# A two-layer decoder trunk on one core: where running sums join the residual, how the first input is loaded, and when heads are transposed

## The chip, the cores and the metric

The kernel runs on one core of a Trainium2 chip. The metric is the device time of one execution in microseconds (us). The kernel before took 2208.25 us, the median of three runs (2207.6, 2208.25 and 2216.12 us).

## What is computed

A residual stream x of 256 positions and 2048 channels (float32) goes through two layers and a final RMSNorm. Cut to what matters here:

```
for l in range(DEPTH):                      # DEPTH = 2
    h    = rms_norm(x, attn_norm_g[l])
    proj = h @ w_in[l]                      # 2048 -> 5632: q, k, v of two attention groups, su, sv
    mix  = concat(moba_attention(...),      # 6 heads of 128
                  diff_attention(...),      # 6 heads, two softmaxes each, RMSNorm per head
                  spatial_gating(gelu(su), gelu(sv)))
    x = x + mix @ w_out[l]
    h = rms_norm(x, mlp_norm_g[l])
    x = x + square(relu(h @ w_mlp_in[l])) @ w_mlp_out[l]     # 2048 -> 8192 -> 2048
return rms_norm(x, final_norm_g)
```

## The kernel before, in words

**Splitting.** Every float32 weight tile is split into a high and a low part of the matmul format (`weights`, lines 102 to 121, and `halves`): ScalarE (ACT) copies the high part, `hi_*`, and VectorE (DVE) subtracts it from the raw tile to give the low part, `lo_*`. Activations are split likewise. A product is then three matmuls of 512 columns: high by high, low by high, high by low. The raw tiles have three buffers, the split ones four of two k steps each, so that the splitting runs ahead of TensorE (PE) by at most eight k steps. All weights are loaded from SyncE's queue (SP).

**The two matmul routines.** `gemm` (line 138) makes 2 x 512 columns of a plain product in two of the four PSUM banks of the pool `psg`. `gemm7` (line 181) makes 2 x 1024 columns with seven products in place of eight for the first 1536 rows of the weights' k range (tiles `b11`, `t1`, `t2`, `b22`, `t3`, `t4`, `b21`), and the remaining rows plainly (`plain`). It uses all four banks, px, py, pz and pw. px and py gather running sums: at four points the running content is saved with `keep` (`s1`, `s5`, `v2`, `v3`), and the bank goes on collecting. At its end the four blocks are the banks plus such saved sums. Between the k steps both routines call `pump()`, which takes one step of a pending generator (`mixing`, the heads, `turn`, `hidden`, `gate`); with two or more pending, the first two take turns.

**The MLP.** The hidden width is cut in four chunks, c = 0 to 3. Each has two `gemm7` of the first matrix (names ending in h) and two of the second (names ending in o), 32 in the two layers, 16 of them o. In an o gemm `keep` (lines 681 to 685) has ACT evict the running sum from PSUM, scaled by `r2` or its negative, to a tile `kept`, and has GpSimd (POOL) start a DMA that adds this tile to the residual `xt` in SBUF. At the end DVE adds each bank times `r2` to `xt` (lines 688 to 691), in the order py, pw, pz, px. In an h gemm `keep` (lines 657 to 663) keeps the sums on chip, and `v3` is a subtraction on DVE, `s5` minus px. The tiles `kept` have four buffers that h and o share.

**The attention part.** For each layer `gemm` first makes the columns sv (line 345 or 354), then the groups 8, 7, ..., 0, 9 of the input projection (`wi`). Between sv and group 8 stand the sums of squares of x, 1/rms (`rstd`), small loads and the eviction of sv's banks (`svz`, line 401). In layer 0 x itself (`xt`, two loads of 1 MB) and the small loads (idt, mask, rope, lng, lnb, lam, swt) stand on SP's queue between the loads of sv and those of group 8. `differential` (line 484) is a generator of six steps for one head: in its fifth step PE multiplies by v, ACT squares, DVE and POOL make 1/rms and ACT scales; in the sixth PE transposes the result (`poT`, line 516).

**The order** of instructions on each engine is fixed at compile time by the framework's scheduler from the order of the program and its own estimates, so an instruction may stand a few places from where the program has it. Each engine works through its own list.

Of the kernel before, what the change touches and what calls it, by code (L numbers as in the profile page):

```python
# [11 lines left out]
AF = mybir.ActivationFunctionType  # L12
ALU = mybir.AluOpType
# [3 lines left out]
P = 128  # L17
# [9 lines left out]
GW = 512  # L27
NG = D // GW
FCH = 4
# [12 lines left out]
def trunk(ctx: ExitStack, tc: tile.TileContext, x_in, xT, w_in, w_out, w_mlp_in, w_mlp_out,  # L42
          cols, sgu_wT, ln_g, ln_b, fin_g, lam, rope, mask, ident, out):
    nc = tc.nc
    V, A, G, T = nc.vector, nc.scalar, nc.gpsimd, nc.tensor
# [22 lines left out]
    def bank(name, tag="m"):  # L68
        return psa.tile([P, GW], F32, tag=tag, name=name)


    xt = [cpool.tile([P, D], F32, name=f"xt{t}") for t in range(2)]
# [61 lines left out]
    def drain():  # L134
        while pending:
            pump()

    def gemm(w, order, c0, lhs, name, sizes=(4, 4, 4, 4), before=None):

        ps = [psg.tile([P, GW], F32, tag="g", name=f"pg{t}_{name}") for t in range(2)]  # L140
        i = 0
        for size in sizes:
            ks = order[i:i + size]
            if before:
                before(ks)
            for k, (hi, lo) in zip(ks, weights(w, ks, c0, f"{name}_{i}")):
                a, j = lhs[k]
                first, last = i == 0, i == len(order) - 1
                i += 1
                for t in range(2):  # L150
                    ah, al = a[:, j, t * P:(t + 1) * P], a[:, j, S + t * P:S + (t + 1) * P]
                    T.matmul(ps[t], lhsT=ah, rhs=hi, start=first, stop=False)  # L152
                    T.matmul(ps[t], lhsT=al, rhs=hi, start=False, stop=False)  # L153
                    T.matmul(ps[t], lhsT=ah, rhs=lo, start=False, stop=last)  # L154
                pump()
        return ps
# [161 lines left out]
    xa = [None] * KT  # L318

    def load_x(ks):  # L320
# [5 lines left out]
        for i, k in enumerate(ks):  # L326
# [2 lines left out]
            split(d[:, k % 2], x0[:, i, :], col(C_ATT + k))  # L329
            xa[k] = (d, k % 2)  # L330

    ss_a = None
    for l in range(DEPTH):
        lam_init = 0.8 - 0.6 * math.exp(-0.3 * l)
        wi, wo, w1, w2 = w_in[l], w_out[l], w_mlp_in[l], w_mlp_out[l]
        allk = list(range(KT))
# [6 lines left out]

        if l == 0:
            psv = gemm(wi, allk, SV * P, xa, "sv0", sizes=(2, 2, 4, 4, 4), before=load_x)
            for t in range(2):
                nc.sync.dma_start(xt[t], x_in[t * P:(t + 1) * P, :])
            nc.sync.dma_start(idt, ident)
            ss_a = sums("a0")
            for t in range(2):  # L350
                for g in range(NG):
                    square_sum(ss_a, t, g, "a0")
        else:
            psv = gemm(wi, allk, SV * P, xa, f"sv{l}")
        drain()
        nc.sync.dma_start(maskt, mask)
        nc.sync.dma_start(ropet, rope)
# [126 lines left out]
        def differential(h):  # L484
            n = f"d{l}{h}"
            qk = turned_qk("d", h, n)
            yield
            e0, s0 = softmax(scores(qk, slice(0, 64), n + "a"), 0.125, n + "a")
            yield
            e1, s1 = softmax(scores(qk, slice(64, 128), n + "b"), 0.125, n + "b")  # L490
            V.tensor_scalar(s1, s1, nlam, None, op0=ALU.mult)
            for j, (a, b) in enumerate(((0, P), (P, 3 * P))):
                A.activation(e0[:, a:b], e0[:, a:b], AF.Copy, scale=s0[:, j:j + 1])
                V.scalar_tensor_tensor(e0[:, a:b], e1[:, a:b], s1[:, j:j + 1], e0[:, a:b],
                                       op0=ALU.mult, op1=ALU.add)
            yield
            pt = probs_t(e0, n)
            vs = vh["d", h]
            yield
            po = bank(f"po_{n}")  # L500
            T.matmul(po[:, 0:P], lhsT=pt[:, 0:P], rhs=vs[0], start=True, stop=True)
            T.matmul(po[:, P:S], lhsT=pt[:, P:S], rhs=vs[0], start=True, stop=False)
            T.matmul(po[:, P:S], lhsT=pt[:, S:3 * P], rhs=vs[1], start=False, stop=True)
            o = t1(f"o_{n}")
            ssq = small.tile([P, 2], F32, tag="ssq", name=f"ssq_{n}")
            for t in range(2):
                A.activation(o[:, t * P:(t + 1) * P], po[:, t * P:(t + 1) * P], AF.Square,
                             accum_out=ssq[:, t:t + 1])
            V.tensor_scalar(ssq, ssq, 1.0 / P, EPS, op0=ALU.mult, op1=ALU.add)
            G.tensor_tensor(ssq, ssq, mhalf[:, :2], op=ALU.pow)  # L510
            for t in range(2):
                A.activation(o[:, t * P:(t + 1) * P], po[:, t * P:(t + 1) * P], AF.Copy, scale=ssq[:, t:t + 1])
            yield
            pT = bank(f"poT_{n}")
            for t in range(2):
                T.transpose(pT[:, t * P:(t + 1) * P], o[:, t * P:(t + 1) * P], idt)
            split(mix_half(6 + h), pT[:, :S], gsub)
# [67 lines left out]

        pending.append(mixing())
        for g in (8, 7, 6, 5, 4, 3, 2, 1, 0, 9):
            ps = gemm(wi, allk, g * GW, xa, f"wi{l}{g}")
            if g == 9:
                pending.append(gate(ps))  # L590
            else:
                take(g, ps)
            for h in {5: (2, 3, 4, 5), 4: (0, 1)}.get(g, ()):
                pending.append(differential(h))
            for h in {1: (4, 5), 0: (0, 1, 2, 3)}.get(g, ()):
                pending.append(block_attention(h))
# [14 lines left out]
        for g in range(NG):  # L611
            ps = gemm(wo, order, g * GW, Late(), f"wo{l}{g}")
# [13 lines left out]
        xa = [None] * KT  # L626
# [25 lines left out]
        for c in range(FCH):  # L652
            hid, hs = [None] * KT, [None] * SP
            for g in range(2):
                kept = {}

                def keep(what, ps, kept=kept, n=f"{l}{c}{g}"):
                    k = mlp.tile([P, GW], F32, tag="kept", name=f"k{what}h{n}", bufs=4)
                    if what == "v3":
                        V.tensor_tensor(k, kept["s5"], ps, op=ALU.subtract)  # L660
                    else:
                        A.activation(k, ps, AF.Copy)
                    kept[what] = k

                ps = gemm7(w1, c * fw + 2 * g * GW, Want(xm), Want(xs), allk[2 * SP:], keep, f"h{l}{c}{g}")
                z11, z12, z22 = kept["s1"], kept["v2"], kept["v3"]
                V.scalar_tensor_tensor(z12, z12, -1.0, ps[0][1], op0=ALU.mult, op1=ALU.add)
                V.tensor_tensor(z22, z22, ps[1][1], op=ALU.add)
                pending.append(hidden(hid, hs, ((z12, z12), (z22, z22)), 8 * g + 4, f"hid{l}{c}{g}b"))
                V.tensor_tensor(z11, z11, ps[0][0], op=ALU.add)  # L670
                pending.append(hidden(hid, hs, ((z11, z11), (ps[1][0], None)), 8 * g, f"hid{l}{c}{g}a"))
                if r2 is None:
                    rm = rstd(ss_m, f"m{l}")
                    r2 = small.tile([P, 4], F32, tag="r2", name=f"r2_{l}", bufs=2)
                    V.tensor_tensor(r2[:, :2], rm, rm, op=ALU.mult)
                    V.tensor_scalar(r2[:, 2:], r2[:, :2], -1.0, None, op0=ALU.mult)
            for g in range(2):
                def xg(t, half, g=g):
                    return xt[t][:, (2 * g + half) * GW:(2 * g + half + 1) * GW]

                def keep(what, ps, g=g, n=f"{l}{c}{g}"):
                    t, half, sign = {"s1": (0, 0, 0), "v2": (0, 1, 2), "s5": (1, 1, 0), "v3": (1, 1, 2)}[what]
                    k = mlp.tile([P, GW], F32, tag="kept", name=f"k{what}o{n}", bufs=4)
                    A.activation(k, ps, AF.Copy, scale=r2[:, sign + t:sign + t + 1])
                    G.dma_start(xg(t, half, g), k, accum_op=ALU.add)

                ps = gemm7(w2[c * fw:(c + 1) * fw], 2 * g * GW, Want(hid), Want(hs), late, keep, f"o{l}{c}{g}")
                for half in (1, 0):
                    for t in range(2):
                        V.scalar_tensor_tensor(xg(t, half), ps[t][half], r2[:, t:t + 1], xg(t, half),  # L690
                                               op0=ALU.mult, op1=ALU.add)
                        if c == FCH - 1:
                            square_sum(ss_a, t, 2 * g + half, f"n{l}")
                    if c == FCH - 1 and not fin:
                        q = 2 * g + half
                        pending.append(turn(xa, xt, q * GW, 4 * q, f"xa{l + 1}_{q}_", C_ATT + (l + 1) * KT))
# [75 lines left out]
```

## Time and profile before

| | before |
|---|---|
| median of 3 runs | 2208.25 us |
| the profiled execution | 2210.08 us |
| its span, first to last instruction | 2208.4 us |
| mean granted TensorE clock | 0.993 |
| PE busy with matmuls | 2148.7 us (97%) |
| DVE busy | 1614.9 us (73%) |
| ACT busy | 1312.5 us (59%) |
| POOL busy | 74.0 us (3%) |
| DMA, mean rate over the span | 191 GB/s |
| HBM read | 402.23 MB |

All times in the profile are microseconds from the start of the span unless they are marked ns. Matmuls overlap, and their ends are modelled: a matmul of 512 columns is recorded as 0.39 us long while the next starts 0.23 us after it. So "busy" is no peak, and a gap of PE between a recorded end and the next start is shorter than the time really lost. [...]

### The profile page before, as it was taken

What the parts mean: (1) busy time and instruction counts of PE and PEld (TensorE: products, weight loads), DVE (VectorE), ACT (ScalarE), POOL (GpSimd) and SP (SyncE); (2) the same over time, 40 slices, a digit from 0 to 9 for tenths busy, and PEclk for the clock granted to TensorE, in tenths of its full rate; (3) what the DMA queues carried; (4) which work ended last, traced back from release to release, by engine and by line L of the source; (5) the groups of instructions that cost most, each with busy time, mean ns of one, the idle gap of its engine ahead of it and who ended that gap; (6) DMA issues with size and microseconds to landing.
All of it is one profiled execution on the core that took longest, in us unless ns stands there. A gap on an engine that the chain in (4) does not pass through costs nothing. (4 is left out here: it accounts for less than half of the span.)

```text
span 2208.4 us, 26211 instructions
## 1 busy us (share of the span) xinstructions
PE 2148.7 (97%) x9596; PEld 1731.0 (78%) x9596; DVE 1614.9 (73%) x2040; ACT 1312.5 (59%) x1935; POOL 74.0 (3%) x90
## 2 busy tenths in 40 slices
PE   8999999999999999999999999999999999999997
PEld 6877888887787787788888778888878877877885
DVE  6555665897788787788765655668868977887876
ACT  6456465675566565566663655656656755755764
POOL 0000000000000000000000000000000000000000
PEclk9999999999999999999999999999999999999999
DMA  8544565467656666657666444645765676566564
GB/s 294 189 153 139 174 221 181 153 189 222 196 194 197 200 200 208 187 185 223 186 205 196 145 152 156 227 143 183 223 204 191 190 227 209 178 200 208 194 214 124
DMA packets 214385, 422.82 MB, mean 191 GB/s; under 512 B 9840, under 2 KB 10480, under 8 KB 213872
## 3 DMA queue, kind: packets, MB, share of 16 engines
q1 hardware_dynamic: 204176, 402.23, 55.5%
q0 software_dynamic: 9216, 16.78, 4.3%
q10 hardware_dynamic: 864, 2.14, 0.3%
q8 instruction: 75, 1.23, 0.2%
q14 instruction: 54, 0.44, 0.1%
HBM read 402.23 MB, written 2.10 MB: 183 GB/s over the span
## 5 line engine op out<-in xcount | busy, mean ns | idle before, releaser
L119 DVE TENSOR_TENSOR lo_wi<-raw_wi,hi_wi 128x1024 fp32r<-128x1024 f32 x160 | 195.6, 1223 | 177.7 <-ACT hi_wi L118 177.5
L118 ACT ACTIVATE hi_wi<-raw_wi 128x1024 fp32r<-128x1024 f32 x160 | 169.1, 1059 | 182.4 <-PE pg_wi L153 176.1
L118 ACT ACTIVATE hi_o<-raw_o 128x1024 fp32r<-128x1024 f32 x160 | 168.5, 1060 | 171.8 <-PE px_o L221 103.3
L152 PE MATMUL pg_wi<-hi_wi,xa 128*128 128x512 f32 x640 | 261.8, 409 | 4.3 <-ACT hi_wi L118 4.3
L154 PE MATMUL pg_wi<-lo_wi,xa 128*128 128x512 f32 x640 | 253.0, 395 | 1.0 <-DVE lo_wi L119 1.0
L153 PE MATMUL pg_wi<-hi_wi,xa 128*128 128x512 f32 x640 | 252.8, 395 | 0.0
L119 DVE TENSOR_TENSOR lo_h<-raw_h,hi_h 128x1024 fp32r<-128x1024 f32 x160 | 193.0, 1222 | 59.5 <-ACT hi_h L118 59.5
L118 ACT ACTIVATE hi_h<-raw_h 128x1024 fp32r<-128x1024 f32 x160 | 168.4, 1058 | 110.5 <-PE px_h L221 58.6
L119 DVE TENSOR_TENSOR lo_o<-raw_o,hi_o 128x1024 fp32r<-128x1024 f32 x160 | 192.3, 1221 | 35.4 <-ACT hi_o L118 35.3
L152 PEld LDWEIGHTS pg_wi<-hi_wi,xa 128*128 128x128 f32 x640 | 121.1, 189 | 34.1 <-issue 7.3
L154 PEld LDWEIGHTS pg_wi<-lo_wi,xa 128*128 128x128 f32 x640 | 121.1, 189 | 26.8 <-DVE lo_wi L119 1.7
L153 PEld LDWEIGHTS pg_wi<-hi_wi,xa 128*128 128x128 f32 x640 | 121.3, 190 | 22.6 <-issue 0.7
L119 DVE TENSOR_TENSOR lo_wo<-raw_wo,hi_wo 128x1024 fp32r<-128x1024 f32 x64 | 78.4, 1225 | 64.3 <-ACT hi_wo L118 64.1
L208 DVE TENSOR_TENSOR rb_h<-rb_h,rb_h 128x1536 f32<-128x1536 f32 x64 | 112.3, 1755 | 1.0
L208 DVE TENSOR_TENSOR rb_o<-rb_o,rb_o 128x1536 f32<-128x1536 f32 x64 | 112.3, 1754 | 0.8
L118 ACT ACTIVATE hi_wo<-raw_wo 128x1024 fp32r<-128x1024 f32 x64 | 67.7, 1058 | 67.6 <-PE pg_wo L153 62.7
L690 DVE SCALAR_TENSOR_TENSOR xt<-pw_o,r,xt 128x512 f32<-128x512 f32 x16 | 12.0, 751 | 89.7 <-DMA xt<-kv3o 89.7
L152 PE MATMUL pg_wo<-hi_wo,mix 128*128 128x512 f32 x192 | 76.3, 397 | 0.0
L154 PE MATMUL pg_wo<-lo_wo,mix 128*128 128x512 f32 x192 | 75.1, 391 | 0.0
L153 PE MATMUL pg_wo<-hi_wo,mix 128*128 128x512 f32 x192 | 74.8, 390 | 0.0
L222 PE MATMUL py_h<-lo_h,xm 128*128 128x512 f32 x160 | 63.5, 397 | 0.5
L220 PE MATMUL py_h<-hi_h,xm 128*128 128x512 f32 x160 | 63.6, 397 | 0.0
(2141 smaller groups left out, 5635.4 us busy)
## 6 DMA issues: line engine op xcount, KB each, us to landing
raw_wi<-w_in SPq DMA_DIRECT2D x80, 1024.0 KB, 5.2
raw_o<-w_mlp_out SPq DMA_DIRECT2D x160, 512.0 KB, 5.1
raw_h<-w_mlp_in SPq DMA_DIRECT2D x64, 1024.0 KB, 5.5
rb_h<-w_mlp_in SPq DMA_DIRECT2D x64, 768.0 KB, 6.5
rb_o<-w_mlp_out SPq DMA_DIRECT2D x64, 768.0 KB, 6.1
raw_wo<-w_out SPq DMA_DIRECT2D x24, 1024.0 KB, 5.2
raw_h<-w_mlp_in SPq DMA_DIRECT2D x32, 512.0 KB, 5.4
raw_wo<-w_out SPq DMA_DIRECT2D x16, 512.0 KB, 5.0
```

Source lines behind the costliest of these rows:

```text
L118: A.activation(hi, raw[:, i:i + n, :], AF.Copy)
L119: V.tensor_tensor(lo, raw[:, i:i + n, :], hi.bitcast(F32), op=ALU.subtract)
L152: T.matmul(ps[t], lhsT=ah, rhs=hi, start=first, stop=False)
L153: T.matmul(ps[t], lhsT=al, rhs=hi, start=False, stop=False)
L154: T.matmul(ps[t], lhsT=ah, rhs=lo, start=False, stop=last)
L208: V.tensor_tensor(dst, dst, src, op=ALU.add)
L220: T.matmul(ps, lhsT=ah, rhs=hi, start=first, stop=False, skip_group_check=True)
L222: T.matmul(ps, lhsT=ah, rhs=lo, start=False, stop=last, skip_group_check=True)
L690: V.scalar_tensor_tensor(xg(t, half), ps[t][half], r2[:, t:t + 1], xg(t, half), op0=ALU.mult, op1=ALU.add)
```

## The change

Three things change.

1. In the o gemms `keep` starts no DMA. `s1` and `v2` are evicted and scaled as before; `s5` is evicted unscaled; at `v3` DVE subtracts px from the kept `s5` tile and ACT scales the difference in place, so three tiles are kept instead of four. At the end, right behind DVE's update of each slice, the kept tile joins the same slice of `xt`: for c = 0 to 2 by the accumulating DMA from POOL (three per gemm, 36 in all, where 64 were), for c = 3 by an addition on DVE (12 in all).
2. Group 8 of the input projection is now issued directly behind sv, ahead of the sums of squares, `rstd`, the small loads and the eviction of sv. In layer 0 `xt` comes in four loads of 512 KB, each just ahead of one of the four weight loads of group 8, in place of two of 1 MB ahead of all four.
3. `differential` has one more, empty step before its transposes: seven steps.

```diff
+    def load_xt(ks):
+        t, h = divmod(ks[0] // 4, 2)
+        nc.sync.dma_start(xt[t][:, h * 2 * GW:(h + 1) * 2 * GW],
+                          x_in[t * P:(t + 1) * P, h * 2 * GW:(h + 1) * 2 * GW])
...
             psv = gemm(wi, allk, SV * P, xa, "sv0", sizes=(2, 2, 4, 4, 4), before=load_x)
-            for t in range(2):
-                nc.sync.dma_start(xt[t], x_in[t * P:(t + 1) * P, :])
+            ps8 = gemm(wi, allk, 8 * GW, xa, "wi08", before=load_xt)
             nc.sync.dma_start(idt, ident)
...
             psv = gemm(wi, allk, SV * P, xa, f"sv{l}")
+            ps8 = gemm(wi, allk, 8 * GW, xa, f"wi{l}8")
         drain()
...
                 A.activation(o[:, t * P:(t + 1) * P], po[:, t * P:(t + 1) * P], AF.Copy, scale=ssq[:, t:t + 1])
+            yield
             yield
             pT = bank(f"poT_{n}")
...
-            ps = gemm(wi, allk, g * GW, xa, f"wi{l}{g}")
+            ps = ps8 if g == 8 else gemm(wi, allk, g * GW, xa, f"wi{l}{g}")
...
-                def keep(what, ps, g=g, n=f"{l}{c}{g}"):
-                    t, half, sign = {"s1": (0, 0, 0), "v2": (0, 1, 2), "s5": (1, 1, 0), "v3": (1, 1, 2)}[what]
+                kept = {}
+
+                def keep(what, ps, kept=kept, n=f"{l}{c}{g}"):
                     k = mlp.tile([P, GW], F32, tag="kept", name=f"k{what}o{n}", bufs=4)
-                    A.activation(k, ps, AF.Copy, scale=r2[:, sign + t:sign + t + 1])
-                    G.dma_start(xg(t, half, g), k, accum_op=ALU.add)
+                    if what == "v3":
+                        k = kept["s5"]
+                        V.tensor_tensor(k, k, ps, op=ALU.subtract)
+                        A.activation(k, k, AF.Copy, scale=r2[:, 1:2])
+                    else:
+                        i = {"s1": 0, "v2": 2, "s5": None}[what]
+                        A.activation(k, ps, AF.Copy, **({} if i is None else {"scale": r2[:, i:i + 1]}))
+                    kept[what] = k
...
                         V.scalar_tensor_tensor(xg(t, half), ps[t][half], r2[:, t:t + 1], xg(t, half),
                                                op0=ALU.mult, op1=ALU.add)
+                        k = kept.get({(0, 0): "s1", (0, 1): "v2", (1, 1): "v3"}.get((t, half)))
+                        if k is not None and c < FCH - 1:
+                            G.dma_start(xg(t, half), k, accum_op=ALU.add)
+                        elif k is not None:
+                            V.tensor_tensor(xg(t, half), xg(t, half), k, op=ALU.add)
```

## Rows read from the trace of the kernel before

**Rows 1.** The page's first part: busy us, share of the span and instructions per engine.

```profile
PE 2148.7 (97%) x9596; PEld 1731.0 (78%) x9596; DVE 1614.9 (73%) x2040; ACT 1312.5 (59%) x1935; POOL 74.0 (3%) x90
```

**Rows 2.** Who PE waited for: total us, times, longest us.

```profile
PE pz_o L222 <- DVE lo_o L119: 28.6, 13, 3.5
PE poT_d L516 <- ACT o_d L512: 6.4, 6, 1.1
PE pg_wi L152 <- ACT hi_wi L118: 4.3, 1, 4.3
PE pg_wi L154 <- DVE lo_wi L119: 1.0, 1, 1.0
```

**Rows 3.** PE in order of time around one pz_o gap: start, us, [idle before].

```profile
513.00 0.39 PE L220 MATMUL pz_o<-hi_o,hid001b 128*128 128x512 f32 x1
513.22 0.39 PE L221 MATMUL pz_o<-hi_o,hid001b 128*128 128x512 f32 x1
516.36 0.50 PE L222 MATMUL pz_o<-lo_o,hid001b 128*128 128x512 f32 x1 [2.75 <-DVE lo_o L119]
```

**Rows 4.** DVE in order of time around the same gap.

```profile
514.42 0.75 DVE L690 SCALAR_TENSOR_TENSOR xt<-pw_o,r,xt 128x512 f32<-128x512 f32 x1 [6.90 <-DMA xt<-kv3o]
515.09 2.35 DVE L119 TENSOR_TENSOR lo_o<-raw_o,hi_o 128x1024 fp32r<-128x1024 f32 x2
```

**Rows 5.** The tile kv3o: its eviction (ns min/median/max), its DMA's time to landing.

```profile
L684 ACT ACTIVATE kv3o<-px_o,r x16: 665/668/668, 505.6 to 2176.7; 128x512 f32<-128x512 f32 x16
...
DMA to landing us min/median/max: 5.3/7.0/8.6
```

**Rows 6.** Who DVE waited for, the second largest line.

```profile
DVE xt L690 <- DMA xt<-kv3o: 89.7, 16, 7.6
```

**Rows 7.** Stretches: length, busy us per engine, PE clock, DMA share, GB/s.

```profile
33.10:43.30 10.20, 7.11 (x16) 5.13 (x17) 9.53 (x27) 6.52 (x9) 2.52 (x1) 0.50 0.56 195
517.80:521.20 3.40, 3.40 (x9) 2.61 (x9) 2.05 (x3) 1.06 (x1) 0.00 (x0) 0.50 0.69 203
```

**Rows 8.** The start: SP, ACT and PE in order of time.

```profile
11.55 0.52 SPq L347 DMA_DIRECT2D xt<-x_in  x1
...
25.20 1.48 SPq L110 DMA_DIRECT2D raw_wi<-w_in  x3
...
30.36 1.31 ACT L401 ACTIVATE svz<-pg_sv,rc_a 128x512 f32<-128x512 f32 x2 [2.57 <-PE pg_sv L154]
...
34.15 3.88 ACT L118 ACTIVATE hi_wi<-raw_wi 128x1024 fp32r<-128x1024 f32 x4
...
35.24 0.80 PE L152 MATMUL pg_wi<-hi_wi,xa 128*128 128x512 f32 x1 [4.30 <-ACT hi_wi L118]
```

**Rows 9.** A stretch of the start with the DMA engines full; columns as in Rows 7.

```profile
20.00:30.00 10.00, 10.00 (x46) 8.29 (x45) 5.21 (x11) 7.67 (x22) 1.30 (x2) 1.00 1.03 399
```

**Rows 10.** One late transposition of a head: ACT, then PE, in order of time.

```profile
150.91 0.27 ACT L507 ACTIVATE o_d<-po_d 128x128 f32<-128x128 f32 x1
...
153.84 0.44 PE L516 MATMUL poT_d<-idt,o_d 128*128 128x128 f32 x2 [1.01 <-ACT o_d L512]
```

**Rows 11.** The tile kv3h: DVE's subtraction in h gemms, and what its engines waited for.

```profile
L660 DVE TENSOR_TENSOR kv3h<-ks5h,px_h x16: 678/685/689, 416.9 to 2089.3; 128x512 f32<-128x512 f32 x16
...
its engine sat idle before it (us, times) until:
who waited for it (us, times):
  PEld px_h L220: 2.4, 8
```

**Rows 12.** An addition to xt on DVE, and DVE in the last gemm's end.

```profile
L615 DVE TENSOR_TENSOR xt<-xt,pg_wo x16: 678/687/689, 322.5 to 1483.9; 128x512 f32<-128x512 f32 x16
...
2195.11 0.75 DVE L690 SCALAR_TENSOR_TENSOR xt<-pz_o,r,xt 128x512 f32<-128x512 f32 x1 [3.04 <-PE pz_o L222]
2195.79 0.75 DVE L690 SCALAR_TENSOR_TENSOR xt<-px_o,r,xt 128x512 f32<-128x512 f32 x1
```

## The prediction, made before the changed kernel ran

> **What bounds the kernel now.** I read the page's first part first. PE is busy for 2148.7 of the span's 2208.4 us, DVE 73%, ACT 59% [rows 1]. So PE sets the time, and only what PE loses can be won: its gaps, and the stretches in which its clock is halved. Next come PE's own waits [rows 2]; the reader should see that they are few and of three kinds, all of which the change touches: 13 waits of pz_o, 28.6 us; 6 waits of the heads' transposes poT_d, 6.4 us; and group 8's first matmuls in layer 0, 4.3 and 1.0 us. The third view is the clock by stretches: until PE ends there are five stretches at half clock, each just behind one of these gaps: 10.2 us at the start, and four of 3.4 us behind four of the 13 pz_o gaps (one is shown) [rows 7].
>
> A recorded gap is too short. Matmuls start 0.22 to 0.23 us apart, but are recorded as 0.39 us long [rows 3]; so a gap costs itself and 0.16 us more.
>
> **Where the pz_o gaps come from.** PE stands 2.75 us before a matmul with a low part, lo_o [rows 3]. DVE makes this tile at 515.09, right behind the update of xt from pw at 514.42, and before that update DVE had been idle for 6.90 us, for the DMA that adds kv3o to the same slice [rows 4]. That happens in all 16 o gemms, 89.7 us of DVE in all, 5.6 on average [rows 6]: the eviction takes 0.67 us, its DMA 5.3 to 8.6 us to land [rows 5]. In 13 of 16 it uses up the stock of split tiles. In the stretch shown, 6.90 of DVE cost PE 2.75 us, so that the stock was worth some 4 us.
>
> **The change, part by part.**
>
> *Sums after the update.* The update no longer waits for any DMA of its own gemm. Gone: 28.6 + 13 x 0.16 = 30.7 us of PE. The four half-clock stretches are filled with matmuls, 3.40 us busy of 3.40 [rows 7], so each costs half of itself, 1.7 us, 6.8 in all; without the gaps ahead of them I expect none. Sum 37.5 us.
>
> What it adds: (a) 16 subtractions on DVE, by 0.685 us as in the h gemms [rows 11], 11 us, beside PE. The new wait is DVE for PE's px at the end of t3. Queued behind it are the low parts of t4 and of the plain steps, for which PE waits. The h gemms have just this instruction at just this place: 16 of them, before none of which DVE was idle; PE's queue of weight loads waited for them 8 times, 0.3 us each [rows 11]. The wait for px to be read exists today with ACT's eviction. So it costs 0 by that row; the other end is that the stall merely moves, 37.5 us, as PE's waits now show. I take 0: same code, same stage, the nearest row. A gain below zero is excluded, since px has to be read either way. (b) ACT's scaling in place instead of an eviction, about equal to 0.67 us, beside PE, but now behind DVE's subtraction; no PE tile waits for it except ACT's next high parts. (c) 36 accumulating DMAs on POOL behind the update. The next instruction on the same slice comes four gemms later, over 160 us (a gemm7 has 183 matmuls by 0.23 us), against 8.6 us of landing: 0. POOL is idle 97% of the time [rows 1]. (d) Kept tiles: three instead of four, but s1 is held to the end of its gemm and its DMA's landing. The next gemm's first three kept tiles find the other buffers; its fourth comes three quarters through, some 30 us later, against 8.6: 0; if that cover were gone, up to 8.6 us of ACT per gemm. (e) 12 additions by 0.69 us [rows 12], 8.2 us of DVE, beside PE, except in the very last gemm: there DVE goes from pz at 2195.11 to px at 2195.79 with PE already done [rows 12], and the addition of s1 stands in between: +0.7 us at the end.
>
> *The start.* PE is done with sv at 30.9 and waits until 35.24 for group 8's first high part [rows 8]. Two things make it late. SP issues xt, idt and six more loads from 11.55 on, and group 8's weights only at 25.20. And ACT evicts and treats sv first, from 30.36, so that its first split for group 8 is at 34.15 [rows 8]. Afterwards the weights stand behind one quarter of xt: 0.5 + 1 MB, 1.57 million bytes at the 399 GB/s of this stretch [rows 9], so a chunk each 3.9 us. They begin at about 20 us, an estimate: what sv needs, 6.3 million bytes, takes 15.8 us at that rate behind a start of some 4. First weights at about 24, the others at 28, 32, 36, while PE needs them at 30.9, 36, 42, 47. The eviction of sv, and the rest, stand behind them. Gone: 4.3 + 0.16 + 1.0, and half of the 7.11 us in which PE works at half clock [rows 7], 3.6: 9.1 us. Moved past on SP: the seven small loads now land at about 40 us; the first that need them (tables, mixing) work beside group 7, from 53 us on. Moved on ACT: eight squares of some 0.8 us beside four chunks of splits, with no PE wait if they stand where their quarter has landed. New: sv's two banks and group 8's two fill all four, so group 7 waits for sv's eviction; that has from about 37 to 53 us. In layer 1 the same eviction is ready when sv is done, with 22 us of cover; without the cover 2 x 0.67 us. Bounds: from -9.1 to +1.4 us. I take -9.1, since each chunk has 7 us or more in hand.
>
> *The heads.* In a pair, the second head's squares wait in ACT's list until 150.91, and its transposition is 1.01 us late at 153.84 [rows 10]; the same in every pair, 6 times. With one more step in each of two heads that take turns, two pumps by 6 x 0.23 us, 2.8 us, are added between multiplication and transposition, more than the longest wait of 1.1. Gone: 6.4 + 6 x 0.16 = 7.4 us. Steps per layer grow from 36 to 42 where groups 4 to 1 offer 64 pumps: none are short. Bounds 0 to -7.4; I take -7.4.
>
> *Sum.* -37.5 - 9.1 - 7.4 + 0.7 = -53.3 us. The span of 2208.4 becomes 2155.1; the profiled execution took 2210.1 (1.7 around the span) and the median of the runs is 2208.25, 1.8 below it. So 2155 us.
>
> **Rivals.**
>
> *The stall stays in part.* DVE now meets px where it met the DMA. For it: the subtraction is one more thing in a strict order. Against: no idle time before it in 16 h gemms [rows 11]. With half of the 37.5 us left: 2174.
>
> *The start doesn't come.* The squares may stand on ACT ahead of splits whose weights have landed, or DMA order may differ from the program's. Against: PE has some 7 us in hand. 2155 + 9 = 2164.
>
> *The edit doesn't do what it says.* If DVE's update, or another instruction ahead of the low parts, still stands for something as late as the DMA was, all 37.5 us stay: 2192; with the start lost as well, 2202, inside no change. Against: the row names this DMA 16 of 16 times [rows 6].
>
> *Slower: DVE stands at the subtraction.* Rows 4 show what a waiting instruction does on DVE: everything behind it, low parts included, stood 6.90 us. [...] The price as a mechanism here: if the subtraction is placed ahead of low parts that PE needs for t4, each microsecond beyond the stock of about 4 is one of PE. At the longest gap of today, 3.5 + 0.16, with a half-clock stretch behind each, 1.7, in all 16 gemms: 86 us instead of 37.5, against 16.5 won elsewhere: +33, 2241. It becomes slower by more than the measurement tells (0.5%, 11 us, here) when PE loses (53 + 11) / 16 = 4 us per gemm, DVE waiting some 8. Against it: again the h gemms.
>
> **How the numbers follow.** Forecast, 0.70: 2155, its own range 2148 (a few of PE's waits below 1 us go too) to 2163 (the heads or half of the half-clock time stay). Part of the stall stays, 0.12: 2174. Start lost, 0.09: 2164. All of the stall stays, 0.03: 2192; with the start lost, 0.03: 2202. Slower, 0.03: 2241. The range takes in the first three, 2148 to 2176. Faster by over 0.5%: 0.94; within: 0.03; slower: 0.03.
>
> **What would show it.** Right: no line of DVE's xt waiting for a DMA; pz_o behind lo_o under 3 us of PE in all; no half clock until PE ends; poT_d gone from PE's waits; PE from sv to group 8 without a gap, group 8 done at about 54 us; 36 accumulating DMAs; 28 more DVE instructions. Wrong: DVE idle before the new subtraction with PE behind it, PE waiting for low parts of t4, for the tile kept, or at group 7's first matmul for sv's banks; or a half-clock stretch without a gap ahead of it, which would mean that the clock has another cause.

## The result, and the profile after

The changed kernel takes 2152.73 us (median of four runs, 2152.22 to 2153.29) against 2207.93 us, a ratio of 0.9742 (95% interval 0.9719 to 0.9765). The forecast was 2155.

| | before | after |
|---|---|---|
| the profiled execution | 2210.08 us | 2153.29 us |
| its span | 2208.4 us | 2151.6 us |
| mean granted clock | 0.993 | 0.998 |
| PE busy | 2148.7 us (97%) | 2133.4 us (99%) |
| accumulating DMAs, MB of their queue | 64, 16.78 | 36, 9.44 |

The page's first part (answering [rows 1]) and all of PE's waits (answering [rows 2]; total us, times, longest us) of the kernel after:

```profile
PE 2133.4 (99%) x9596; PEld 1728.5 (80%) x9596; DVE 1632.3 (76%) x2068; ACT 1312.2 (61%) x1935; POOL 48.8 (2%) x62
```

```profile
PE pg_sv L152 <- ACT hi_sv L118: 1.6, 1, 1.6
PE pw L82 <- DVE warm L76: 1.5, 1, 1.5
PE py_o L222 <- DVE lo_o L119: 0.5, 1, 0.5
```

All three kinds of waits are gone. What is left is the first 7 us of the program and one wait of 0.5 us. DVE has 28 instructions more, as the edit says, and is 17.4 us busier; PE is 15.3 us less busy with the same 9596 matmuls, for the greater part because it no longer works at half clock behind the gaps (7.1 us of the first stretch in [rows 7] and four stretches like the second, 20.7 us of busy time at a granted clock of 0.50, about half of which full clock would have saved: in the second stretch matmuls start 0.43 us apart, and 0.23 where the clock is 1.00).

DVE in order of time (start, duration, instruction; a bracket at a line's end would tell the idle time ahead of it and who ended it) in the first o gemm, some 487 to 503 us in the kernel after, the stretch that answers to [rows 4]:

```profile
490.82 0.75 DVE L704 SCALAR_TENSOR_TENSOR xt<-py_o,r,xt 128x512 f32<-128x512 f32 x1
491.51 0.75 DVE L704 SCALAR_TENSOR_TENSOR xt<-pw_o,r,xt 128x512 f32<-128x512 f32 x1
492.37 1.23 DVE L119 TENSOR_TENSOR lo_o<-raw_o,hi_o 128x1024 fp32r<-128x1024 f32 x1
493.61 0.69 DVE L694 TENSOR_TENSOR ks5o<-ks5o,px_o 128x512 f32<-128x512 f32 x1
494.21 1.82 DVE L166 TENSOR_TENSOR lo_t4o<-rb_o,hi_t4o 128x1024 fp32r<-128x1024 f32 x2
```

No bracket stands at the end of any of these lines: DVE waited for nothing. pw's update now follows py's at once. The new subtraction stands one low part later and finds px ready.

Where the time went, stage by stage. Both kernels make the same number of matmuls of 512 columns in the same order of stages, so the stages can be cut by counting them, and the difference of the times at the cuts gives each stage's share (worked out from the starts of the matmuls in both traces):

| stage | change, us | forecast |
|---|---|---|
| sv of layer 0 | +1.0 | 0 |
| group 8 of layer 0 (mixing's 16 small matmuls, 1.85 us, leave it) | -10.9 | -9.1 - 1.85 |
| groups 7 to 9 of layer 0, with the heads | -1.85 | -3.7 + 1.85 |
| group 8 of layer 1 (mixing leaves it too) | -2.9 | -1.85 |
| groups 7 to 9 of layer 1, with the heads | -2.1 | -3.7 + 1.85 |
| the 12 o gemms of c = 0 to 2 | -38.85 | -36.1 |
| the 4 o gemms of c = 3 | -2.4 | -1.4 |
| all h gemms and output projections | +0.1 | 0 |
| behind the last matmul | +1.1 | +0.7 |
| sum | -56.8 | -53.3 |

The sv stage is 1.0 us later because matmuls that start 0.43 us apart, against 0.23 later, go on until 13.0 us in this execution (its granted clock is recorded as 1.00 there), and in the profiled one of before only in places up to some 7.5 us. This varies from execution to execution: in six others of kernels that have the same start the stage ends 0.6 to 1.2 us earlier than here, in `after_again` 0.1.

### The profile page after: what moved, and what is told of

It is laid out like the page before. It is cut to its first block, busy times and chain, and to the rows that moved or that the text cites. A ratio compares the mean times of both kernels' runs of the same rounds, so it can differ in the third digit from the quotient of the medians.

```text
span 2151.6 us, 26174 instructions
## 1 busy us (share of the span) xinstructions
PE 2133.4 (99%) x9596; PEld 1728.5 (80%) x9596; DVE 1632.3 (76%) x2068; ACT 1312.2 (61%) x1935; POOL 48.8 (2%) x62
## 3 DMA queue, kind: packets, MB, share of 16 engines
q0 software_dynamic: 5184, 9.44, 2.5%
q8 instruction: 75, 1.23, 0.2%
## 4 chain that ended last, share of the span: by engine, by line
PE 84%; issue 9%; DVE 4%; ACT 2%; DMA 0%; ACTq 0%; POOL 0%; POOLq 0%; SPq 0%; DVEq 0%
PE pg_wi L152 7%; PE pg_wi L154 7%; PE pg_wi L153 7%; PE pg_wo L152 3%; PE pg_wo L153 3%; PE pg_wo L154 3%; PE px_o L177 2%; PE px_o L176 2%; PE px_o L175 2%; PE px_o L220 2%; PE py_o L220 2%; PE pw_o L220 2%; PE py_o L222 2%; PE pw_o L222 1%; PE pw_o L221 1%
## 5 line engine op out<-in xcount | busy, mean ns | idle before, releaser
L220 PE MATMUL pw_h<-hi_h,xm 128*128 128x512 f32 x160 | 63.3, 396 | 0.0
```

The source lines that it names most:

```text
L220: T.matmul(ps, lhsT=ah, rhs=hi, start=first, stop=False, skip_group_check=True)
```

## The experiments

Each kernel ran beside the kernel before. That kernel's own runs vary from 2204 to 2220 us (more on this at the end), so differences of a few us are taken between kernels that vary less, or from traces.

**The three parts, each alone.** `p1_sums`, `p2_start` and `p3_heads` are the kernel before with one part of the diff each.

> The kernel before with the first part alone: the kept sums join the residual behind the update, with the subtraction on DVE. Theory (the DMA wait of DVE and the half-clock stretches behind it): 37.5 us less, 0.7 more at the end, so about 2171 us, with the start's gap and the six late transpositions of heads still there. Rival (the parts are not independent; the stalls removed by one part only move the others): clearly less than 37 us here, and the three parts alone don't add up to the whole, 55 us.

2170.11 us (2169.25 to 2170.44), ratio 0.9810 (0.9789 to 0.9832): 40.7 us less. PE's waits in this run show the pz_o line gone and the other two kinds untouched:

```profile
PE poT_d L516 <- ACT o_d L512: 6.4, 6, 1.1
PE pg_wi L152 <- ACT hi_wi L118: 4.3, 1, 4.3
```

> The kernel before with the second part alone: group 8 issued directly behind sv, x in quarters beside its weights. Theory: 9.1 us less in layer 0 and up to 1 in layer 1, about 2198 us; PE goes from sv to group 8 without a gap and without a half-clock stretch. Rival (a later wait takes the gain back, at group 7 for sv's banks): about 2208 us.

2201.45 us (2196.08 to 2204.29), ratio 0.9953 (0.9937 to 0.9969): 9.4 us less. In the trace group 8 of layer 0 ends 10.9 us earlier, of which 1.85 are mixing's matmuls that move to group 7; 9.1 us stay at the end of group 9. Layer 1 gives 1.0. PE's later waits show none for sv's banks.

> The kernel before with the third part alone: one more step ahead of a head's transposes. Theory: the six waits of about 1.06 us and 0.16 us each go, 7.4 us less, about 2200.5 us. Rival (the stall only moves to another instruction of the heads): 2208 us, with new waits of PE in the same stretch.

2201.92 us (2199.29 to 2210.61), ratio 0.9958 (0.9942 to 0.9974): 8.9 us less. By the trace the two attention parts end 3.7 and 3.9 us earlier; the line poT_d is gone from PE's waits and no other of the heads is in its place.

The medians' gains add up to 59 us, where the whole gave 55 to 56. In the traces, the first part counted at PE's end and the other two in the stages of the attention parts alone, they are 41.4 + 10.1 + 7.6 = 59.1 us, against 57.9 for the whole at PE's end, and 1.0 of that difference is the slow start named above. The o gemms, which the second and the third part leave as they were, are left out for these two: by the half-clock stretches of the one execution profiled they are 3.9 us longer in `p2_start` and 1.5 shorter in `p3_heads`. So the parts add up, to about 1 us in the traces and to 3 or 4 in the medians.

**Which transfer stalled DVE.** `v3_behind` moves one of the four DMAs of each o gemm:

```diff
+                    if what == "v3":
+                        kept[what] = k
+                    else:
                         G.dma_start(xg(t, half, g), k, accum_op=ALU.add)
...
                                                op0=ALU.mult, op1=ALU.add)
+                        if (t, half) == (1, 1):
+                            G.dma_start(xg(t, half), kept["v3"], accum_op=ALU.add)
```

> The kernel before with one transfer moved: only v3's accumulating DMA is issued behind the update of pw; s1, s5 and v2 are evicted and added as before, and there is no subtraction on DVE. Theory (the stall is the wait for v3's DMA alone): as much as the whole first part, 37 us less, about 2171 us. Rival (the next DMA in line takes its place: v2's lands a median 7.3 us after its issue, just as the update of py wants its slice): half of the stall or more stays, 2190 us or above, with DVE's update of py waiting for kv2o.

2170.91 us (2170.62 to 2171.07), ratio 0.9814 (0.9793 to 0.9836): within 0.8 us of the whole first part. The v3 DMA is as slow as before (median to landing, last column), yet nothing stands behind it:

```profile
xt<-kv2o POOLq DMA_DIRECT2D x16, 256.0 KB, 7.3
xt<-kv3o POOLq DMA_DIRECT2D x16, 256.0 KB, 7.1
```

Beside constants, DVE waits for one DMA in this run, once and for 0.3 us: py's update for kv2o. All 64 transfers are still made, so their number was not what cost the time. The stall was the place of one transfer out of four, and its length did not matter once nobody waited for it.

**The subtraction on DVE.** `no_subtract` is the changed kernel with ACT evicting all four sums into four kept tiles; all join behind the update:

```diff
-                    if what == "v3":
-                        k = kept["s5"]
-                        V.tensor_tensor(k, k, ps, op=ALU.subtract)
-                        A.activation(k, k, AF.Copy, scale=r2[:, 1:2])
+                    A.activation(k, ps, AF.Copy, scale=r2[:, sign + t:sign + t + 1])
```

> The changed kernel with the subtraction on DVE undone: ACT evicts all four running sums, scaled, into four kept tiles, and each joins its slice behind the update (four accumulating DMAs per gemm for c = 0 to 2, sixteen additions on DVE in all for c = 3). Theory (what counts is that no transfer stands ahead of the update; the subtraction is free and worth nothing by itself): as the changed kernel, within 3 us of 2153. Rival (four tiles held to the end of the gemm use up the four buffers, so that the next gemm's first kept sums wait for a DMA to land, up to 8.6 us in each of 12 gemms): 2170 us or more, with ACT's ks1 waiting for a DMA.

2154.64 us (2153.97 to 2154.81), 1.9 us above the changed kernel, so the first theory. In the traces the 16 o gemms are 2.0 us longer together, but not where the subtraction was taken away: in the 12 gemms of c = 0 to 2 PE comes back to px 1.19 us after its last start in t3, against 1.18 in the changed kernel. Of the 2.0 us, 1.2 stand at PE's first matmuls into py behind s5, 0.1 us in most gemms. There the edit changes one thing more: it evicts s5 scaled, as before, where the changed kernel evicts it unscaled. The eviction (ns min/median/max) and PE's weight loads that waited for it (us, times), first in this kernel, then in the changed one:

```profile
L693 ACT ACTIVATE ks5o<-py_o,r x16: 674/680/697, 472.0 to 2101.2; 128x512 f32<-128x512 f32 x16
  PEld py_o L220: 3.1, 12
```

```profile
L698 ACT ACTIVATE ks5o<-py_o x16: 578/592/602, 473.1 to 2100.6; 128x512 f32<-128x512 f32 x16
  PEld py_o L220: 1.9, 8
```

`v3_behind`, which also keeps the scaled eviction, loses the same 1.1 us at py in the gemms of c = 0 to 2. The other 0.7 us stand in the four gemms of c = 3, most of it at px, where PE's matmuls have another order. So at px the subtraction on DVE is worth next to nothing, in the gemms of c = 0 to 2 at least; the eviction without a scale, some 0.09 us shorter, frees py that much sooner. The kept tiles held to the end cost nothing that can be seen: no ACT instruction waits for one.

**How much more DVE could take.** `dve_dose` and `dve_dose16` add 8 and 16 multiplications of the kept tile by one behind the subtraction.

```diff
                         V.tensor_tensor(k, k, ps, op=ALU.subtract)
+                        for _ in range(8):                 # 16 in dve_dose16
+                            V.tensor_scalar(k, k, 1.0, None, op0=ALU.mult)
```

> The changed kernel with eight more DVE instructions behind v3's subtraction in each of the 16 o gemms, multiplications of the kept tile by one, 0.48 us each by the final scaling's rows: 3.8 us per gemm, 61 us of DVE in all, beyond what the kernel needs. DVE is idle for 8 of the 43 us of an o gemm. Theory A (only DVE's total matters while PE is fed): less than 3 us more, 2153 to 2156 us. Theory B (DVE's work is free only as far as the stock of split tiles, some 4 us, at the place where it stands): still near nothing, up to 10 us more. If the time grows by 30 us or more, both fall and the added subtraction was not free either.

> As the run before with sixteen such instructions, 7.7 us per gemm, just what DVE has idle in one. Theory A (the total): DVE is nearly full, PE is fed most of the time: up to 15 us more, below 2170 us. Theory B (the stock at the place): 7.7 less 4 are 3.7 us of PE in each of 16 gemms, and half-clock stretches behind them, 60 to 86 us more, 2213 us or above: slower than the kernel before.

2153.47 us (2153.0 to 2153.66) with eight, 0.7 us more; 2167.34 us (2167.24 to 2169.1) with sixteen, 14.6 us more. The dose was smaller than stated: an added instruction is recorded at 0.42 us, and the next one starts 0.34 us after it where that is another tile's and 0.46 where it is the next multiplication; by these starts sixteen take 6.5 us of DVE per gemm and eight 3.2. DVE's busy time in one o gemm of 43.1 us (stretch, then PE, PEld, DVE, ACT, POOL) with sixteen and in the changed kernel:

```profile
466.70:509.80 43.10, 43.10 (x197) 35.05 (x196) 40.47 (x51) 27.14 (x36) 1.92 (x2) 1.00 0.64 203
```

```profile
466.70:509.80 43.10, 43.10 (x196) 35.09 (x195) 35.14 (x37) 27.81 (x36) 1.93 (x2) 1.00 0.68 206
```

So sixteen add 5.3 us of busy time and eight 2.8, less than by the starts, since the recorded ends of neighbours overlap. Theory A holds for both: with DVE 94% busy PE loses 0.8 us at 13 of the 16 gemms. It does so at the head of the next gemm, in a recorded wait of 0.5 us for ACT's high parts, which in turn wait for a sum of two raw tiles on DVE. The largest single loss, 4 us of the 14.6, is at the head of the very last gemm, where DVE also adds the kept sums of c = 3 and ACT has the squares. Theory B, that work beyond a stock of about 4 us is paid in full, falls: with the 6.5 us that were really added it asks for 2.4 us in each gemm, some 38 in all, and at the low parts of t4, where PE waits nowhere in this run. The added work isn't one wait. It stands between the low parts in DVE's list, one to four instructions at a time, and they stay ahead of PE; the wait of 6.90 us in [rows 4] stood in one place.

**What closed the gap at the start.** `x_whole` loads x in two pieces ahead of group 8's weights; `sp_order` puts x and all seven small loads ahead of them, as before the change.

> The changed kernel with x in two loads of 1 MB ahead of all of group 8's weights, in place of quarters beside them; the small loads stay behind. Theory (PE has some 7 us in hand): first weights 4 us later, at 28 us, still ahead of PE at 31: no change, 2153 us. Rival (the quarters are what takes the gap away): a gap of PE at group 8 of 1 us or more and up to 3 us for the clock behind it, 2156 us or above.

2154.01 us (2153.59 to 2154.18), 1.3 us more, between the two: the rival's gap is there, 1.1 us of PE at group 8, but no half-clock stretch behind it. ACT in order of time, first in this run, then in the changed kernel:

```profile
27.13 0.62 ACT L297 ACTIVATE sq_a<-xt 128x512 f32<-128x512 f32 x1
27.65 0.19 ACT L297 ACTIVATION_READ_ACCUMULATOR sq_a<-xt 128x1 f32 x1
30.52 0.69 ACT L407 ACTIVATE svz<-pg_sv,rc_a 128x512 f32<-128x512 f32 x1 [2.68 <-PE pg_sv L154]
31.10 2.00 ACT L118 ACTIVATE hi_wi<-raw_wi 128x1024 fp32r<-128x1024 f32 x2
```

```profile
24.53 0.19 ACT L297 ACTIVATION_READ_ACCUMULATOR sq_a<-xt 128x1 f32 x1
24.87 1.06 ACT L118 ACTIVATE hi_wi<-raw_wi 128x1024 fp32r<-128x1024 f32 x1 [0.16 <-DMA raw_wi<-w_in]
...
40.71 1.27 ACT L407 ACTIVATE svz<-pg_sv,rc_a 128x512 f32<-128x512 f32 x2 [1.28 <-POOL rc_a L303]
```

With the quarters the first split stands at 24.87, just after its weights. With x ahead of the weights these land at 27.9 us (issued at 14.47, 13.4 to landing), as the theory has it. But the scheduler has the eviction of sv before the first split, which so begins only at 31.10, with ACT idle for 2.68 us before it.

> The changed kernel with the loads of the start in the order of before on SP's queue: xt in two loads of 1 MB, idt and the six other small loads all ahead of group 8's weights in layer 0; the squares and sv's eviction stay behind group 8 on the engines. It separates the two causes of the gap at the start. Theory A (the late weights): they land at 32 us as before, the first split ends at 33, so some 2 of the 4.3 us gap come back and most of a half-clock stretch, 4 to 6 us more than the changed kernel. Theory B (ACT's squares and eviction ahead of the splits): no gap worth naming, within 1 us of it. By A 2157 to 2159 us, by B 2153 us.

2161.29 us (2161.06 to 2161.6), 8.5 us more: nearly all of the start's gain is lost, more than theory A's 4 to 6. PE waits 4.30 us as in [rows 8], and a half-clock stretch of 6.8 us follows. The weights are issued at 25.84 and ACT's list is back in the order of before, the eviction of sv and its gelu ahead of the first split:

```profile
33.11 1.30 ACT L310 ACTIVATE svu<-svu 128x512 f32<-128x512 f32 x2
34.31 1.99 ACT L118 ACTIVATE hi_wi<-raw_wi 128x1024 fp32r<-128x1024 f32 x2
```

The run does not separate late weights from ACT's order as it was meant to, since the order of ACT's list moved with the loads. The landings on record bound the two: group 8's first weights land at 33.2 us here (7.4 after their issue) and at 32.0 in the kernel before (25.20 and 6.8), so ACT's list held the first split up by 1.1 us here and by some 2 there. The rest of the 4.3 us, 3.2 here and about half there, is late weights. In `x_whole` it is the other way round, and the wait of 1.1 us is ACT's list alone. The order of the loads decides both.

**The additions of c = 3.** `c3_dma` uses the DMA for c = 3 too; `c3_early` adds the sums on DVE ahead of the update, when they are kept.

> The changed kernel with the accumulating DMA for c = 3 too, in place of the twelve additions on DVE. Theory: in the last gemm of the second layer the sums of squares wait for s1's DMA, which lands 3 to 9 us after the update: the end is later by about 6 us less the 0.7 of the addition, about 2158 us; at the end of the first layer the same wait is beside eight k steps of sv and costs nothing. Rival (the landing is hidden by the output's own transfers): 2152 us, as much less as the addition took.

2164.4 us (2162.83 to 2167.38), 11.7 us more, twice what was expected. At the end the squares wait for s1's DMA, as told.

```profile
2149.15 0.63 ACT L297 ACTIVATE sq_n<-xt 128x512 f32<-128x512 f32 x1 [10.25 <-DMA xt<-ks1o]
```

It costs less than told: the time behind the last matmul is 2.4 us more than in the changed kernel, where some 5 were expected. The rest was not foreseen: squares that wait for a DMA (13.8 us in three waits for ks5o's) stand on ACT ahead of high parts, and the last chunk of each layer loses 3.0 to 3.6 us; at the start of layer 1 PE's transposes wait 1.7 us for the same DMA.

> The changed kernel unaltered, for comparison with the next run on the same chip: 2152.7 us again, within 0.6 of it.

2152.78 us (2152.24 to 2153.6, six runs).

> The changed kernel with the twelve additions of c = 3 ahead of the update instead of behind it: each kept sum is added to its slice by DVE as soon as it is kept. Theory: the addition of s1 leaves the end, where it stands between the last matmul and the last squares: 0.7 us less, 1.1 at most, about 2151.8 us, and no new wait, since the sum is kept on chip some 10 us or more ahead of the update. Rival (the additions now meet ACT's scaling of v3 just ahead of the update of pw, and DVE stands again): the same time or more, with DVE waiting for ACT's ks5o in two gemms per layer.

2153.93 us (2153.7 to 2154.49, five runs), 1.15 us more: the rival's time, but not its mechanism, since DVE waits nowhere for ks5o in this run. The time behind the last matmul is 12.5 us against 13.7, so the addition did leave the end. But ahead of it the last two gemms are 2.2 us longer together, 1.7 of it in the last one, with waits that the changed kernel doesn't have there:

```profile
PE py_o L220 <- ACT ks5o L698: 0.7, 1, 0.7
PE pw_o L220 <- ACT hi_o L118: 0.3, 1, 0.3
```

The order around the earlier additions is another, and the last two gemms cost more than the end gives; which instruction of that order is to blame was not tested. No version here beats the changed kernel.

## Why the prediction was right, step by step

**The pz_o gaps.** Right in mechanism, a little low in size: 41.2 us (38.85 + 2.4) where 37.5 were forecast; `p1_sums` alone shows 40.9. By the starts of the matmuls 1.5 us of the difference come from the price of a gap: the prediction adds 0.16 us to a recorded one, but the matmul behind it, 0.50 us long [rows 3], also holds the next up by 0.11, so that a gap costs 0.27 us more than is recorded, in 13 of them. Some 1.3 us are terms that the prediction left out, small waits of PE for py: the changed kernel evicts s5 unscaled, 0.09 us faster, which `no_subtract` shows. The rest, 0.9 us, is in the gemms of c = 3: two waits at the head of the last gemm are gone (1.4 us by the starts), and a new one of 0.5 stands in another. The prediction's exclusion, "a gain below zero is excluded, since px has to be read either way", holds where it was made: in 12 of the 16 gemms PE comes back to px 0.01 us sooner than with the subtraction undone, and no more.

The stock of some 4 us is confirmed more closely than the prediction could show it from one gap. In the kernel before, 12 of the 13 recorded gaps of PE are DVE's wait for kv3o less 4.15 us, from 5.62 and 1.47 us to 7.64 and 3.49, and the 13th is its wait less 3.91. The three waits that cost PE nothing were the shortest, 3.18, 2.72 and 1.48 us.

**The subtraction, and the rival on the slower side.** Taking the h gemms as the nearest row was right: no idle time of DVE ahead of the new subtraction. What stood behind pw's update on DVE in the kernel before stood with it for 6.90 us [rows 4]. Nothing had to wait behind the subtraction: in the first o gemm pw's update (0.75 us) and a low part (1.23 us) stand ahead of it, px is ready when it comes, and DVE waits for px in none of the 16 gemms. What the runs narrow is the price named for it, a stock of 4 us: it is a price for a wait, not for work, of which 6.5 us per gemm cost 0.8.

**The half-clock stretches.** Right: none from the slow start, which ends at 13.1 us in the changed kernel and at 10.6 in `dve_dose`, to PE's end; neither has a recorded gap of PE above 0.5 us in between.

**The start.** 9.1 us forecast, 9.1 in `p2_start`. But the reason for it was half right: "PE has some 7 us in hand" was true of the landing of the weights, not of ACT's list, as `x_whole` shows by 1.3 us. The quarters are worth that; the order of all the loads is worth the rest, as `sp_order` shows. The new need for four banks cost nothing: sv's eviction stands at 40.71, group 7 begins at 53.

**The heads.** 7.4 forecast, 7.6 measured alone.

**The end.** +0.7 forecast, +1.1 measured. The addition of s1 was thought to stand between the two updates. It stands behind both, and the squares of that slice come later still, so that the size came out nearly right with the order wrong:

```profile
2137.25 0.75 DVE L704 SCALAR_TENSOR_TENSOR xt<-pz_o,r,xt 128x512 f32<-128x512 f32 x1 [3.50 <-PE pz_o L222]
2137.93 0.75 DVE L704 SCALAR_TENSOR_TENSOR xt<-px_o,r,xt 128x512 f32<-128x512 f32 x1
2138.59 0.68 DVE L710 TENSOR_TENSOR xt<-xt,ks1o 128x512 f32<-128x512 f32 x1
```

**The sum.** -53.3 forecast, -56.8 in the spans: 3.7 us more were won in the first part and 1.2 more in layer 1, most of it where mixing's matmuls no longer wait (0.8 us of PE before, left out of the sum); 1.0 was lost to PE's slow start and 0.4 at the end.

## What to carry to other kernels

Look for an engine that stands for a transfer while the tiles it makes for the bound engine lie behind it, as DVE did for 6.90 us in [rows 4]: moving one DMA to the other side of the instruction that waited gave as much as the whole rewrite of the part (2170.91 us against 2170.11). Work that has no wait in it filled this engine far at little cost (88% busy for 0.7 us in all, 94% for 0.8 us in most gemms of 43), while each wait of 5.1 to 7.6 us here cost 1.2 to 3.5 us of the bound engine, and those up to 3.2 us cost nothing. And where a compiler orders the lists, moving loads can move the order of other engines too, as it moved ACT's in `sp_order`, so a place that nobody edited must be read again after each edit.

## What the hardware showed that was not expected

The kernel before varies from execution to execution, 2205.1 to 2218.1 us in 17 runs beside each other, at mean granted clocks of 0.990 to 0.995; kernels without the pz_o gaps hold within 2 us (2152.2 to 2153.6 in all ten runs of the changed kernel, 2169.25 to 2170.44 for `p1_sums`), while `p2_start` and `p3_heads`, which keep the gaps, spread over 8 and 11 us, and `c3_dma`, which has new ones of up to 1.1 us and a half-clock stretch in its profiled execution, over 4.5. In the profiled execution of before half the clock followed four of 13 gaps, for 3.4 us each. In that of `p2_start` it followed six, three times for 3.4 and three times for 6.8 us, one of each here:

```profile
550.40:553.80 3.40, 3.40 (x9) 2.63 (x10) 2.71 (x3) 0.00 (x0) 0.00 (x0) 0.51 0.35 67
1639.30:1646.10 6.80, 6.02 (x14) 4.76 (x15) 4.28 (x5) 1.06 (x1) 0.00 (x0) 0.50 0.52 163
```

That is 30.6 us at half clock against 13.6, with the gaps themselves 2.7 us shorter, 25.9 in all. The length of a gap did not decide it: in the profiled execution of before a recorded gap of 1.96 us (at 918 us) was followed by a stretch and one of 3.49 (at 560 us) was not. What decides it was not tested. In these runs a kernel with many such gaps pays for them in one execution and not in another, and taking the gaps out took out the spread too.
